# A decoder layer on one core: low parts of weights on VectorE, another pace of the inverse, tied gates, and other places for sums and tiles

## The chip, the cores and the metric

The kernel runs on one core of a Trainium2 chip. The metric is the device time of one execution in microseconds. The core has TensorE (PE; its weight loads are PEld), VectorE (DVE), ScalarE (ACT), GpSimd (POOL) and SyncE (SP), which run their own instruction queues and wait for one another by semaphores. DMAs are issued from the queues of SP, ACT and POOL.

## The reference

One layer of a decoder trunk, for 1024 positions of width 1024, in float32 (cut to what matters):

```python
h = rms_norm(x, norm1_g);  proj = h @ w_in
p_rwkv, p_sb, q_mem, gate_logits = split(proj)
y_a = rwkv7_branch(p_rwkv)                 # 8 heads x 64, delta-rule state, recurrence over time
y_b = stick_breaking_branch(p_sb)          # 8 heads x 64, strictly causal
y_m = memory_branch(q_mem, mem)            # 4 heads x 128, softmax over 256 memory tokens
gates = sigmoid(gate_logits)               # 3 branches x 1024
x = x + sum_b(gates_b * (y_b @ w_branch_b)) @ w_out
x = x + conv_ffn(x)                        # up 1024 -> 5632, causal depthwise conv of 3, silu(gate) * val, down 2816 -> 1024
```

## The kernel before, in words

**High and low parts.** TensorE multiplies in the fp32r format. Each operand is split into a high part (a copy rounded to fp32r, made on ScalarE) and a low part (the operand minus the high part). Every product is three matmuls: high by high, high by low, low by high (`mm3`, L102). For a weight, `split_raw` (L82) makes the high part `wh` on ScalarE (L83) and the low part `wl`, usually on GpSimd (L89); with `dve=True` it is made on VectorE (L86), behind the last fixed VectorE instruction. `split_w` (L96) loads a weight block of 128 x 1024 into a buffer `wr` and calls `split_raw`; `wr`, `wh` and `wl` have two buffers each.

**Order.** `pinned` (L119) keeps the instructions that go through it in program order on their engine and records the last one of each engine in `last_fixed`. `behind` (L127) puts one instruction after another on the same engine. All other instructions are placed by a scheduler, by priority. TensorE's order is that of the program.

**Fillers and main work.** A stream of items (`stream`, L852) is the filler: projections of the stick-breaking keys and queries, the gates (`gate_item`, L871), the memory's keys and values, the memory queries, later the branch products. An item is a block of 48 matmuls (8 steps of six) with hooks at some steps; the next item's weight is loaded and split when an item starts. `weave` (L1945) alternates the steps of a main generator with filler steps. Main generators are, in order, `rwkv_prep` (four pairs of heads p), `sb_attn` (stick-breaking attention, the first attention), `mem_attn` (attention to the memory, the second), `stage2` (the RWKV recurrence) and `group_norm`.

- `rwkv_prep` (L411): `decayed` (L528) is a product on GpSimd whose result TensorE transposes in `turned`.
- `sb_qk` (L891) gives, for a pair p of heads, a key item, a sum of squares of the keys (`k_ss`), a query item and hooks for the gate item behind it. `k_bc` broadcasts the keys' factors over TensorE (the transposed tile comes from `expand_heads`, L358), `k_split` makes high and low parts of the keys, `q_ss` sums the queries' squares on TensorE and calls `head_norm` (L816), which takes the sums out of a PSUM bank (`hn`, L822) and has GpSimd raise them to a power (L190).
- `sb_attn` (L953): for each of 64 units TensorE forms scores, ScalarE takes a sigmoid (L971), VectorE runs a scan (L977), TensorE transposes, ScalarE copies, TensorE multiplies by the values.
- `inverse` (L573): 62 steps of two VectorE instructions (L580, L582) invert triangular blocks in place, then 16 DMAs on GpSimd's queue (L589) write the result (`td`), with three generator steps for each. `run` advances it by `pace[0]` tenths of a step for each filler step: 8 from the first attention on. What is left of it is done behind the mark "mem". `stage2` reads `td`.
- `mem_attn` (L1183): for each of 8 units scores, a maximum on VectorE (L1201), an exponential on ScalarE (L1207), scaling, transposes and the product with the values.
- A gate item ends with two copies out of PSUM on ScalarE (L877), a product on VectorE (L878), later a sigmoid and a store.

**The feed-forward layer.** Up and down projections save multiplications by a two-by-two block scheme with seven products in place of eight. In `up_phase` (L1509) a pair n of column blocks has the products 1, 5, 6, 2, 7, 4, 3 (`step`), of 12 matmuls each; L1677 adds product 6 to a partial sum and so frees the bank that product 7 accumulates into; `conv` applies the convolution; `act_sums` (L1636) forms sums of the activated blocks (L1638) in a tile `sa` and stores them, a "not late" and a "late" half. `hl` (L1543) makes high and low parts of weight sums in tiles of tag `l4`, of which there are 16. In `down_phase` (L1806) each of the seven products is 11 steps f of 12 matmuls; `prep` loads and splits the operands three steps ahead (L1843 to L1846), `complete` adds the last sums into the residual tiles at the steps f = 0 to 3 of the next product, and `release` issues the stores at f = 5.

## Time and profile before

| | |
|---|---|
| runs shown | 1799.64, 1798.66, 1793.97 us (median 1798.66) |
| profiled execution | 1796.01 us; span from the first to the last instruction 1794.2 us |
| mean granted TensorE clock | 0.999 |
| TensorE, VectorE, ScalarE, GpSimd busy | 1778.1, 1176.6, 882.9, 737.2 us |
| first attention, main part | about 317 to 640 us from the span's start |
| second attention | about 671 to 745 us |
| recurrence on TensorE | from 792.6 us |
| up phase, down phase | about 1156 to 1580, 1580 to 1790 us |

A row of a profile gives a line of the kernel, an engine, an operation, the tile written <- the tiles read, and times in us unless marked ns. The ends of matmuls are modelled, so TensorE counts as busy for a little longer than it works. In a list of waits "PE g L117 <- DVE hn L822" reads: TensorE, about to write a tile g at L117, waited for VectorE's instruction on tile hn at L822.

### The profile page before, as it was taken

The page shows a single profiled execution, that of the slowest core. Times are in us where ns is not written, and L with a number is a line of the kernel's source. Part 1 is how long each engine was busy: PE and PEld are TensorE (multiplying, and loading weights), DVE is VectorE, ACT ScalarE, POOL GpSimd, SP SyncE. Part 2 cuts the span into 40 slices and gives each one's busy share as a digit, 9 for nine tenths or more (in the row PEclk, how much of TensorE's full clock was granted, in tenths as well). Part 3 has the DMA queues.
Part 4 walks back from the last instruction along what each step waited for, and adds up shares of the span by engine and source line. Part 5 has one row for each costly group of instructions (what it writes and reads, how often), then busy time and mean ns, then how long its engine had stood idle before and what let it go on. Part 6 is the DMA issues. An engine that isn't in the chain of part 4 may idle for free.

```text
span 1794.2 us, 27468 instructions
## 1 busy us (share of the span) xinstructions
PE 1778.1 (99%) x10481; PEld 1444.7 (81%) x10481; DVE 1176.6 (66%) x1670; ACT 882.9 (49%) x1667; POOL 737.2 (41%) x426
## 2 busy tenths in 40 slices
PE   9999999999999999999999999999999999999999
PEld 7777777878788887787777888887888888888887
DVE  5666655898987415233533782697767777785596
ACT  6544344465666636534556534464444445444343
POOL 1233252322222443122333321347777677635454
PEclk9999999999999999999999999999999999999999
DMA  4256574111111342557764662323322323396475
GB/s 185 73 168 194 177 252 133 55 53 45 51 59 65 124 144 68 181 184 252 275 232 162 224 215 102 118 89 123 100 88 98 120 91 120 112 324 225 143 245 201
DMA packets 120757, 263.39 MB, mean 147 GB/s; under 512 B 28329, under 2 KB 41129, under 8 KB 120498
## 3 DMA queue, kind: packets, MB, share of 16 engines
q1 hardware_dynamic: 82434, 193.31, 32.7%
q10 hardware_dynamic: 34416, 55.72, 8.5%
q0 software_dynamic: 3776, 12.62, 2.1%
q8 instruction: 82, 1.34, 0.3%
q14 instruction: 49, 0.40, 0.1%
HBM read 180.04 MB, written 81.53 MB: 146 GB/s over the span
## 4 chain that ended last, share of the span: by engine, by line
PE 90%; DVE 4%; POOL 2%; issue 1%; ACT 1%; DMA 1%; SPq 0%; ACTq 0%; DVEq 0%; POOLq 0%
PE mm L134 74%; PE g L134 13%; PE g L117 4%; POOL dw L1846 1%; DVE at L977 1%; DVE it L580 1%; DVE inst L582 1%; DMA at<-in_xT_dram 0%; DVE qk L923 0%; DVE qk L922 0%; DMA wr<-in_w_in_dram 0%; POOL wl L89 0%; DVE w L911 0%; POOL hf L190 0%; DMA qk<-vd 0%
## 5 line engine op out<-in xcount | busy, mean ns | idle before, releaser
L89 POOL TENSOR_TENSOR wl<-wr,wh 128x1024 fp32r<-128x1024 f32 x75 | 189.0, 2521 | 434.6 <-ACT wh L83 434.5
L134 PE MATMUL mm<-xhi,wh 128*128 128x512 f32 x784 | 261.2, 414 | 0.6 <-ACT w L928 0.4
L134 PE MATMUL mm<-xlo,wh 128*128 128x512 f32 x784 | 244.1, 393 | 0.2
L134 PE MATMUL mm<-xhi,wl 128*128 128x512 f32 x784 | 242.8, 391 | 0.2 <-POOL wl L89 0.2
L134 PEld LDWEIGHTS mm<-xlo,wh 128*128 128x128 f32 x784 | 147.4, 188 | 33.5 <-DVE xlo L219 1.0
L134 PEld LDWEIGHTS mm<-xhi,wl 128*128 128x128 f32 x784 | 147.5, 188 | 33.2 <-POOL wl L89 0.6
L134 PEld LDWEIGHTS mm<-xhi,wh 128*128 128x128 f32 x784 | 137.3, 190 | 30.5 <-issue 7.9
L83 ACT ACTIVATE wh<-wr 128x1024 fp32r<-128x1024 f32 x75 | 79.5, 1060 | 89.8 <-PE mm L134 67.5
L134 PE MATMUL mm<-dw,da 128*128 128x512 f32 x528 | 120.9, 390 | 0.0
L134 PE MATMUL mm<-BT,l 128*128 128x512 f32 x504 | 117.9, 390 | 0.3 <-POOL l L1547 0.3
L134 PEld LDWEIGHTS mm<-dw,da 128*128 128x128 f32 x528 | 99.0, 188 | 21.3 <-DVE da L1845 0.8
L1846 POOL TENSOR_TENSOR dw<-draw,dw 128x512 fp32r<-128x512 f32 x55 | 82.6, 1514 | 77.3 <-ACT dw L1844 76.0
L134 PEld LDWEIGHTS mm<-BT,l 128*128 128x128 f32 x504 | 94.6, 188 | 20.2 <-POOL l L1547 0.7
L134 PE MATMUL mm<-BT,wh 128*128 128x512 f32 x352 | 108.6, 390 | 1.7 <-DVE u L1677 1.7
L134 PE MATMUL mm<-B,wh 128*128 128x512 f32 x352 | 108.6, 390 | 0.0
L977 DVE TENSOR_TENSOR_SCAN at<-at,at 128x128 f32<-128x128 f32 (+3 forms) x64 | 91.1, 1428 | 23.3 <-ACT at L971 23.0
L1845 DVE TENSOR_TENSOR da<-draw,da 128x512 fp32r<-128x512 f32 x77 | 68.1, 894 | 50.4 <-ACT da L1843 50.0
L190 POOL TENSOR_TENSOR hf<-rs,half 128x16 f32<-128x16 f32 (+1 forms) x18 | 49.3, 2738 | 105.4 <-DVE rs L187 100.6
L134 PE MATMUL g<-dw,da 128*128 128x512 f32 x396 | 90.5, 390 | 0.4 <-POOL dw L1846 0.4
L1843 ACT ACTIVATE da<-draw 128x512 fp32r<-128x512 f32 x77 | 48.3, 629 | 82.6 <-PE mm L134 34.1
L134 PEld LDWEIGHTS g<-dw,da 128*128 128x128 f32 x396 | 74.3, 188 | 16.1 <-POOL dw L1846 0.8
L878 DVE TENSOR_TENSOR w<-w,rbc 128x1024 f32<-128x1024 f32 x24 | 48.3, 2012 | 56.1 <-ACT w L877 56.0
(342 smaller groups left out, 3963.4 us busy)
## 6 DMA issues: line engine op xcount, KB each, us to landing
wr<-in_w_in_dram SPq DMA_DIRECT2D x49, 512.0 KB, 3.8
draw<-actd SPq DMA_DIRECT2D x77, 256.0 KB, 3.0
at<-scr SPq DMA_DIRECT2D x28, 512.0 KB, 5.5
draw<-in_w_down_dram SPq DMA_DIRECT2D x55, 256.0 KB, 4.5
rw<-in_w_up_dram SPq DMA_DIRECT2D x22, 512.0 KB, 3.5
actd<-gall ACTq DMA_DIRECT2D x41, 256.0 KB, 3.2
gsd<-w ACTq DMA_DIRECT2D x20, 512.0 KB, 2.8
wr<-in_w_up_dram SPq DMA_DIRECT2D x18, 512.0 KB, 3.6
```

Of the source, the lines that this page charges most:

```text
L83: ins = self.nc.scalar.activation(hi, raw, AF.Copy)
L89: self.nc.gpsimd.tensor_tensor(lo, raw, hi.bitcast(F32), ALU.subtract)
L117: self.pinned(self.nc.tensor.transpose(out, in_, self.ident[:n, :n]))
L134: self.pinned(self.nc.tensor.matmul(*a, **k))
L190: nc.gpsimd.tensor_tensor(out, t[:, :n], self.half[:, :n], ALU.pow)
L580: self.pinned(nc.vector.tensor_tensor(tv, X[:, 0:s, s : s + 1].to_broadcast([128, s, n]), X[:, s : s + 1, s + 1 : 64].to_broadcast([128, s ...
L582: self.pinned(nc.vector.tensor_tensor(X[:, 0:s, s + 1 : 64], X[:, 0:s, s + 1 : 64], tv, ALU.add))
L878: nc.vector.tensor_tensor(g, g, self.rbc, ALU.mult)
L977: self.pinned(nc.vector.tensor_tensor_scan(sn[:, :W][:, ::-1], sn[:, :W][:, ::-1], self.smask[:, 1024 - W :][:, ::-1], 1.0, ALU.mult, ALU. ...
L1843: self.pinned(nc.scalar.activation(A[:, 0], a, AF.Copy))
L1845: self.pinned(nc.vector.tensor_tensor(A[:, 1], a, A[:, 0].bitcast(F32), ALU.subtract))
L1846: nc.gpsimd.tensor_tensor(Wt[:, 1], w, Wt[:, 0].bitcast(F32), ALU.subtract)
```

## The change

- `split_w` hands `low_dve` on to `split_raw`. It is set by a new entry of the item list, between the second and the third of the gates that follow the four key and query pairs, and taken back behind the mark "mem".
- `decayed` of the last pair (p = 3) is put behind the newest low part made on GpSimd.
- In the second attention (`late`) a gate's copies and its product go behind the last fixed instruction of their engine.
- For pair 0 `k_bc`, `k_split(0)` and `q_ss` come one step of six matmuls later.
- The inverse runs at 6 tenths from the first attention on and at 11 from the second on.
- `hl` for 512 columns puts both parts into one tile. The sums of the activated blocks 0 and 1 are formed at other products.
- In the down phase `complete` runs at f = 0, 2, 4, 6 and `release` at f = 8.

```diff
@@ split_raw
-            self.nc.gpsimd.tensor_tensor(lo, raw, hi.bitcast(F32), ALU.subtract)
+            self.last_wl = self.nc.gpsimd.tensor_tensor(lo, raw, hi.bitcast(F32), ALU.subtract)
         return hi, lo
+
+    def last(self, ins):
+        if self.late:
+            self.behind(ins, self.last_fixed[ins.ins.engine])
+        return ins
@@ split_w
-        return self.split_raw(raw, hi, lo)
+        return self.split_raw(raw, hi, lo, self.low_dve)
@@ startup
+        self.late = self.low_dve = False
@@ rwkv_prep, decayed
-            nc.gpsimd.tensor_tensor(
+            ins = nc.gpsimd.tensor_tensor(
                 self.c8(bp), self.c8(bk), pc[:, h * 8 : h * 8 + 8].unsqueeze(2).to_broadcast([128, 8, 128]), ALU.mult)
+            if p == 3:
+                self.behind(ins, self.last_wl)
@@ gate_item, fin
-                self.leave(nc.scalar.activation(g[:, h * 512 : (h + 1) * 512], pp[h], AF.Copy))
-            nc.vector.tensor_tensor(g, g, self.rbc, ALU.mult)
+                self.leave(self.last(nc.scalar.activation(g[:, h * 512 : (h + 1) * 512], pp[h], AF.Copy)))
+            self.last(nc.vector.tensor_tensor(g, g, self.rbc, ALU.mult))
@@ sb_qk
-        hooks = {1: lambda: k_split(1), 3 if p else 2: q_ss, 4: lambda: q_split(0), 6: lambda: q_split(1)}
-        kq = {4: k_bc, 5: lambda: k_split(0)}
+        hooks = {1: lambda: k_split(1), 3: q_ss, 4: lambda: q_split(0), 6: lambda: q_split(1)}
+        kq = {4: k_bc, 5: lambda: k_split(0)} if p else {5: k_bc, 6: lambda: k_split(0)}
@@ up_phase, hl
-            hi, lo = (pool.tile([128, n], F32R, name=self.nm(t), tag=t, bufs=16 if t == "l4" else 2) for t in tags)
+            if n == 512:
+                t = pool.tile([128, 2, n], F32R, name=self.nm("l"), tag="l4")
+                hi, lo = t[:, 0], t[:, 1]
+            else:
+                hi, lo = (pool.tile([128, n], F32R, name=self.nm(t), tag=t, bufs=16 if t == "l4" else 2) for t in tags)
@@ up_phase, step 6
                 if n > 2 and pairs[n - 1][2]:
-                    act_sums(pairs[n - 1][1], True)
+                    act_sums(pairs[n - 1][1], n > 4)
@@ up_phase, step 3
-                elif pairs[n][2]:
+                elif pairs[n][2] and n > 3:
                     act_sums(pairs[n][1], False)
@@ up_phase, loop over pairs
-                elif n == 3 and i in (5, 6, 7, 4):
-                    late, part = ((False, 0), (False, 1), (True, 0), (True, 1))[(5, 6, 7, 4).index(i)]
-                    act_sums(0, late, (part,))
+                elif n == 3 and i == 5:
+                    act_sums(0, False, (0,))
+                elif n == 3 and i == 6:
+                    act_sums(0, False, (1,))
+                    act_sums(0, True, (0,))
+                elif n == 3 and i == 7:
+                    act_sums(0, True, (1,))
+                elif n == 4 and i == 7:
+                    act_sums(1, True)
@@ down_phase
-            if f < 4:
-                complete(f)
-            elif f == 5:
+            if f < 8 and f % 2 == 0:
+                complete(f // 2)
+            elif f == 8:
                 release()
@@ run
-        items += [gate({0: prep[0], 5: prep[1]}), gate(), gate({2: prep[0], 6: prep[1]}), mss, *mv, *mk, mqi[0][0], mark("kv")]
+        items += [gate({0: prep[0], 5: prep[1]}), gate(), lambda: setattr(self, "low_dve", True), gate({2: prep[0], 6: prep[1]}), mss, *mv, *mk, mqi[0][0], mark("kv")]
...
-        pace[0] = 8
+        pace[0] = 6
         self.guard = True
         need("sb0")
         self.weave(self.sb_attn(qk, need), pump, 1.03, 0)
+        pace[0] = 11
         need("kv")
+        self.late = True
         self.weave(self.mem_attn(mq, need), pump, 1.6, 0)
         need("mem")
-        self.guard, self.last_fin = False, None
+        self.guard, self.last_fin, self.late, self.low_dve = False, None, False, False
```

## The prediction

> **What bounds the kernel now.** I read the page first, then the list of who waited for whom on TensorE, then the waits' own stretches.
>
> ```profile
> span 1794.2 us, 27468 instructions
> PE 1778.1 (99%) x10481; PEld 1444.7 (81%) x10481; DVE 1176.6 (66%) x1670; ACT 882.9 (49%) x1667; POOL 737.2 (41%) x426
> ```
>
> TensorE is busy for 1778.1 of 1794.2 us, and the change neither adds nor removes a matmul. So what can be won is only the time in which TensorE stands still. The waits of TensorE, longest first (engine and line that waits, whom it waited for, total us, times, longest), are these:
>
> ```profile
> PE g L117 <- DVE hn L822: 1.8, 1, 1.8
> PE mm L134 <- DVE u L1677: 1.7, 1, 1.7
> PE g L134 <- DVE hn L822: 1.5, 1, 1.5
> PE g L134 <- DVE qk L196: 1.5, 1, 1.5
> PE mm L134 <- POOL wl L89: 1.5, 2, 1.3
> PE g L117 <- DVE w L358: 0.7, 1, 0.7
> PE g L134 <- ACT at L1207: 0.6, 1, 0.6
> PE g L134 <- ACT w L929: 0.5, 1, 0.5
> PE mm L134 <- DVE qk L1171: 0.5, 1, 0.5
> PE g L134 <- DVE ys L648: 0.5, 1, 0.5
> PE mm L134 <- ACT w L928: 0.4, 1, 0.4
> PE g L134 <- POOL dw L1846: 0.4, 1, 0.4
> PE mm L134 <- POOL l L1547: 0.3, 1, 0.3
> ```
>
> They add up to 11.9 us in 14 waits, and each belongs to one place of the code. L196 (start), L1171 and L648 lie where the change does nothing: 2.5 us stay. To the other 9.4 us comes one stretch of slow clock. The columns are the stretch, its length, busy us (instructions) of TensorE, its weight loads, VectorE, ScalarE and GpSimd, granted clock, DMA share and GB/s:
>
> ```profile
> 676.40:679.90 3.50, 2.86 (x44) 2.31 (x43) 1.11 (x3) 3.06 (x8) 1.11 (x2) 1.00 0.55 143
> 679.90:683.40 3.50, 3.50 (x12) 2.83 (x12) 2.85 (x10) 0.95 (x3) 1.23 (x1) 0.51 0.14 49
> ```
>
> Right behind the 0.6 us wait for L1207 the clock is 0.51 for 3.5 us, which loses about 3.5 x 0.49 = 1.7 us. The ceiling of the whole change is so 9.4 + 1.7 = 11.1 us, 0.6% of the time.
>
> **The change part by part.**
>
> *GpSimd's order at the last RWKV pair* (`decayed` for p = 3 goes behind the newest weight's low part).
>
> ```profile
> 245.85 1.90 POOL L530 TENSOR_TENSOR it<-qk,pc 128x1024 f32<-128x1024 f32 x1 [6.40 <-DVE qk L417]
> 247.71 5.69 POOL L89 TENSOR_TENSOR wl<-wr,wh 128x1024 fp32r<-128x1024 f32 x2
> 258.49 1.03 PE L117 MATMUL g<-kon,it 128*128 128x128 f32 x8
> ```
>
> The 1.90 us product stands ahead of the low part for which TensorE waits 1.3 us. With the two exchanged that wait goes. The product then ends about one low part later, near 250, and its reader on TensorE comes at 258.49, so 8 us of projection hide it. **-1.3 us.**
>
> *The hooks of pair 0* (key broadcast, key split and query sum each one step of six matmuls later).
>
> ```profile
> 439.70 1.38 PE mm L134 x6
> 319.72 0.35 ACT L971 ACTIVATE at<-g,nf 128x128 f32<-128x128 f32 x1
> 324.89 0.42 DVE L977 TENSOR_TENSOR_SCAN at<-at,at 128x128 f32<-128x128 f32 x1
> ```
>
> A step of six is 1.38 us, longer than the 0.7 (L358) and 0.5 us (L929) that TensorE waits there: both go. What is late next is the query's factor, up to 1.38 us later: the first sigmoid (319.72) waits for it, but the scan that reads it starts 5 us later, held by VectorE's own queue. **-1.2 us.**
>
> *Fewer early inverse steps* (0.6 instead of 0.8 per step of the filler in the first attention, 1.1 in the second). The chain of the work that ended last, cut to the stretches ahead of the two waits for L822, has these shares by line (27 us from 436, 28 us from 358):
>
> ```profile
> by line: DVE it L580 20.3%; PE mm L134 19.9%; DVE at L977 18.8%; DVE inst L582 12.6%; DVE qk L923 9.1%; DVE qk L922 8.6%; DVE w L911 5.2%; PE g L117 2.9%; PE g L134 2.0%; issue 0.7%; DVE hn L822 0.4%
> by line: DVE at L977 29.3%; DVE it L580 18.4%; DVE inst L582 18.2%; DVE qk L923 8.8%; DVE qk L922 8.4%; DVE w L911 4.6%; DVE qk L939 4.6%; PE g L134 4.3%; DVE w L358 2.5%; PE g L117 1.2%; issue 0.9%; DVE hn L822 0.7%
> 316.00:600.00 284.00, 280.33 (x1923) 228.90 (x1921) 245.03 (x224) 169.98 (x322) 69.01 (x30) 1.00 0.18 58
> ```
>
> VectorE is busy for 245 of 284 us there, and hn, a tiny operation that frees a PSUM bank, stands behind its backlog. The inverse (L580 and L582) is 32.9% of 27 us = 8.9 us of the one chain and 36.6% of 28 = 10.2 us of the other. A quarter less takes 2.2 and 2.6 us out, more than the 1.8 and 1.5 us waited. **-3.3 us.** The 0.4 us for L928 (ScalarE) stays.
>
> The steps moved have to be done before the recurrence reads the inverse:
>
> ```profile
> L580 DVE TENSOR_TENSOR it<-inst x62: 226/945/3359, 284.3 to 588.0; 128x62 f32<-128x62 f32 x2, 128x122 f32<-128x122 f32 x2, 128x180 f32<-128x180 f32 x2, 128x236 f32<-128x236 f32 x2
> L589 POOL DMA_DIRECT2D td<-inst x16: 796/832/913, 588.9 to 699.8; - x16
> 792.59 0.52 PE L134 MATMUL g<-qk,at 64*64 64x64 f32 x12
> ```
>
> At 0.6 the 303.7 us of VectorE's part become 405. The first attention ends near 640 with 88% of it done, and the last 15 of 124 instructions follow at 1.1 by about 667. The 16 transfers behind them (48 steps, now 111 us at 0.8) take 81 at 1.1 and end near 748. The first reader comes at 792.59, so 45 us of filler hide this; without the cover the recurrence would start late by the same amount.
>
> *Low parts of the weights on VectorE.* The switch is set behind the third gate from the last key/query pair, so it covers the memory's eight half-products, four query projections and four gates, 16 low parts from about 600 on. "Both attentions" is thus the end of the first and the second; in most of the first GpSimd keeps them.
>
> ```profile
> L89 POOL TENSOR_TENSOR wl<-wr,wh x75: 2360/2401/3891, 41.4 to 1044.8; 128x1024 fp32r<-128x1024 f32 x75
> L230 DVE TENSOR_TENSOR wl<-wr,wh x2: 1218/1222/1227, 6.1 to 9.9; 128x1024 fp32r<-128x1024 f32 x2
> 600.00:785.00 185.00, 183.73 (x1119) 149.98 (x1118) 64.84 (x111) 90.86 (x180) 65.21 (x44) 0.99 0.43 138
> ```
>
> GpSimd loses 16 x 2.40 = 38.4 us, VectorE gets 16 x 1.22 = 19.5 us, in a stretch where it is idle for 120 us. Each low part is ready 1.2 us sooner, so the remaining 0.2 us of TensorE's waits for L89 goes. Against it stands a new wait: VectorE takes its queue in order, and a low part that stands there before its high part is copied holds the attention's maxima and scans behind it. Nothing in the trace shows this exactly; the bounds are 0 and 19.5 us (every one exposed in full). The nearest row is the query's low part, which waits for ScalarE in the same way: 8 of L1171 in this stretch cost TensorE 0.5 us in all. I take twice that for 16: **-0.2 + 1.0 us.**
>
> The rule against this part is in the Trainium skill, "TensorE: Matmul & The Clock Gate", section "Architectural detail": ScalarE and VectorE are strict FIFOs. The first rival below is what it would do here.
>
> *Tied gates* (in the second attention copies and products of a gate follow the last fixed instruction of their engine). Behind a late copy waits the next user of its two PSUM banks. The row for L928, 0.4 us for such a copy, over three gates gives 0 to 1.2 us; ScalarE is 49% and VectorE 35% busy there, so I take 0. As nothing then gets ahead of the attention's exponentials, the 0.6 us for L1207 goes, and with it the window that fell to 2.86 busy us of 3.5: **-0.6 - 1.7 us.** The same page, section "What's actually happening", wants a wholly idle window of some 3.4 us before the clock is halved. Here a window with 82% busy came before it, so the measured drop decides; by the rule the wait did not cause it, the 1.7 us stay and the sum below is 1.7 us smaller.
>
> *Up phase.* The chain ahead of the wait for L1677:
>
> ```profile
> 1242.96 1.98 DVE gall L1638
> 1246.56 0.69 DVE u L1677
> 1237.00:1265.00 28.00, 26.01 (x114) 21.00 (x113) 25.29 (x36) 13.27 (x19) 24.57 (x16) 1.00 0.40 132
> ```
>
> Sums of blocks 0 and 1 (L1638) lie together ahead of the L1677 that frees the bank. The change takes block 0's last sums one product earlier and block 1's behind L1677. That clears the 3.6 us between the two rows against 1.7 waited. What is late next are the additions at L1690, with a product of 12 matmuls (2.76 us) as cover. The halves hl makes for 512 columns take one slot of 16 instead of two, so the low part at L1547 need not wait for a slot. **-1.7 - 0.3 us.**
>
> *Down phase.* In the stretch ahead of the wait for L1846 VectorE has no idle time:
>
> ```profile
> 1732.40:1746.40 14.00, 14.00 (x64) 11.59 (x63) 13.86 (x17) 4.62 (x8) 6.19 (x4) 1.00 0.67 224
> ```
>
> Two final sums in each of four successive steps make 13.86 us of work where four steps of twelve matmuls last 4 x 2.76 = 11.0. In every second step they fit. **-0.4 us.** The results leave three steps (8 us) later, two steps ahead of the next loads into their tiles; I take 0, and 0 to 3 us as the price if they collide.
>
> *Sum:* -1.3 - 1.2 - 3.3 - 0.2 + 1.0 - 0.6 - 1.7 - 2.0 - 0.4 = **-9.7 us.** The profiled execution took 1796.0 us (its span and 1.8 around it), so 1786.3. It lies 2.7 below the median of the three runs (1793.97 to 1799.64); the mean of all four is 1797.1. I add that 1.1: **1787.5 us.**
>
> **The rivals.**
>
> *Slower: low parts at the head of VectorE's queue.* Each may wait there for its high part (about 1.06 us on ScalarE, after TensorE has left the buffer) and then run 1.22 us, while maxima and scans wait and TensorE runs out of its four "g" banks. For it speaks that TensorE has no slack in this stretch (183.73 of 185), against it the 120 idle us of VectorE and only 0.5 us lost to L1171. At 2.28 us for half of the 16 it costs 18 us instead of 1: 1787.5 + 17 = 1804.5. It makes the kernel slower from about 1 us per low part on.
>
> *The waits of the first attention come back.*
>
> ```profile
> 394.47 3.36 DVE L580 TENSOR_TENSOR it<-inst 128x962 f32<-128x962 f32 x1
> 394.31 2.49 POOL L89 TENSOR_TENSOR wl<-wr,wh 128x1024 fp32r<-128x1024 f32 x1 [4.42 <-ACT wh L83]
> ```
>
> GpSimd's low parts stay in most of that attention, and an inverse step that runs beside one lasts 3.36 us, where the median was 0.945. If this backlog, not the number of steps, makes hn late, 3.3 us return, and with the clock's 1.7 the kernel takes 1792.5. It is also the case in which the change does less than it says.
>
> *More slow windows of the clock.* Rearranged small matmuls may drop the clock elsewhere, 1.7 us each: with the one kept and two new ones, 1787.5 + 5.1 = 1792.6.
>
> **How the numbers follow.** About 0.3% (5.4 us) can be told from no change, so faster means below 1793.3 and slower above 1804.1. The forecast has 0.62 (1782 to 1792), the returning waits 0.22, the clock 0.07, the queue's head 0.09. Of the second half ends above 1793.3, of the third two parts of seven, of the first 0.02, of the last 0.01 stays below 1804.1: faster 0.76, within 0.16, slower 0.08. The range from 1780 (the ceiling of 11.1 us from 1794, with 3 us for what restarts cost) to 1797 leaves out the queue's case and a tail of the second.
>
> **What would show it.** In the profile after: no wait for L89 near 250, none for L358 and L929 near 300, none for hn; the wait for L1677 and the one for dw gone; clock 1.00 near 680; 16 low parts of about 1.22 us on VectorE between 600 and 790; last td transfer before 760. I am wrong if TensorE shows new waits for VectorE's maxima or low parts between 600 and 790, or for hn at other pairs.

## The result and the profile after

The changed kernel took 1800.70 us (median of 10 runs, 1800.02 to 1802.16), the kernel before 1797.04 us (10 runs, 1793.97 to 1799.64): ratio 1.0023, 95% interval 1.0013 to 1.0032. It is slightly slower, 13 us from the 1787.5 forecast and above the range. Of 71 executions of the kernel before that were timed beside the experiments below, 23 had a mean granted TensorE clock below 1.000 and took 2.8 us longer in the median; of the ten of the changed kernel none had. The profiled execution of the changed kernel took 1800.42 us. The top of its page:

```profile
span 1798.6 us, 27428 instructions
PE 1779.3 (99%) x10481; PEld 1440.9 (80%) x10481; DVE 1191.4 (66%) x1687; ACT 881.3 (49%) x1667; POOL 700.6 (39%) x409
```

The same 10481 matmuls; GpSimd lost 36.6 us of work and VectorE got 14.8. Lines below L89 are shifted: L134 is now L139, L1547 L1559, L1638 L1650, L1677 L1689, L1845 L1863. The longest of TensorE's waits:

```profile
PE mm L139 <- DVE u L1689: 5.8, 7, 0.8
PE mm L139 <- POOL l L1559: 1.5, 1, 1.5
PE g L139 <- DVE qk L202: 1.5, 1, 1.5
PE mm L139 <- POOL wl L1559: 1.4, 1, 1.4
PE mm L139 <- DVE da L1863: 1.2, 1, 1.2
PE mm L139 <- DVE wl L86: 0.7, 2, 0.5
PE g L122 <- ACT at L997: 0.6, 1, 0.6
PE mm L139 <- DVE xlo L225: 0.6, 1, 0.6
```

Both waits for hn are gone, and so are those for L358, L929, L89, L1207 and dw. In their place stand nine waits in the up phase (8.7 us: the rows for L1689 and L1559), one in the down phase (da, L1863) and three short ones in the attention part (L86 and L997, 1.3 us). Where the time went is seen best by comparing the start of the matmul of the same number in TensorE's order in the two traces (after minus before, us; the times are those of before):

| up to | 251 | 303 | 580 | 638 | 699 | 1224 | 1552 | 1750 | end |
|---|---|---|---|---|---|---|---|---|---|
| offset | -1.4 | -2.5 | -7.1 | -4.7 | -7.2 | -7.4 | +3.5 | +2.8 | +4.4 |
| gained or lost in the stretch | -1.4 | -1.1 | -4.6 | +2.4 | -2.5 | -0.2 | **+10.9** | -0.7 | +1.6 |
| forecast | -1.3 | -1.2 | -3.3 | +0.8 | -2.3 | 0 | **-2.0** | -0.4 | 0 |

The first 1224 us went much as forecast (-7.4 against -7.3). The up phase, forecast as a gain of 2.0, lost 10.9 us. The -2.3 forecast up to 699 holds the 1.7 us of the slow clock.

**What happens in the up phase.** Pair 10, before, on ScalarE, GpSimd and VectorE in turn (start us, us, engine line operation, out<-in; in brackets the idle time ahead and who ended it). Product 6 ends at 1358.95, where the first matmul of product 2 starts; product 7 follows 12 matmuls later, at 1361.67 in this trace:

```profile
1358.98 1.06 ACT L1546 ACTIVATE l<-it 128x1024 fp32r<-128x1024 f32 x1 [2.78 <-PE mm L134]
```

```profile
1360.12 2.40 POOL L1547 TENSOR_TENSOR l<-it,l 128x1024 fp32r<-128x1024 f32 x1 [5.29 <-ACT l L1546]
```

```profile
1358.55 1.42 DVE L1638 TENSOR_TENSOR gall<-gall 128x512 f32<-128x512 f32 x2
1359.90 0.68 DVE L1677 TENSOR_TENSOR u<-mm,p 128x512 f32<-128x512 f32 x1
```

The same pair after, where that end lies at 1354.04:

```profile
1346.18 1.05 ACT L1558 ACTIVATE l<-it 128x1024 fp32r<-128x1024 f32 x1
```

```profile
1354.12 2.40 POOL L1559 TENSOR_TENSOR l<-it,l 128x1024 fp32r<-128x1024 f32 x1 [5.62 <-PE mm L139]
```

```profile
1353.56 3.51 DVE L1650 TENSOR_TENSOR gall<-gall 128x512 f32<-128x512 f32 x2
1357.00 0.68 DVE L1689 TENSOR_TENSOR u<-mm,p 128x512 f32<-128x512 f32 x1
```

ScalarE's high part of the weight sums goes 8 us before the end of product 6 instead of right behind it, so GpSimd's low part begins 0.08 us behind that end instead of 1.17. VectorE forms two sums there; the second now begins 0.16 us behind the start of GpSimd's low part and ends 0.5 us behind its end: the two sums took 1.42 us and take 3.51. The u addition behind them frees the bank for product 7. It now ends at 1357.68, product 7 starts at 1357.74, and TensorE has waited. It happens in seven of the eight even pairs from 6 to 20, those whose sums stand there; the waiting product starts about 0.98 us late each time, and such a pair takes 20.4 us where it took 19.05 (shorter delays where one product follows another make the rest). In the eighth, pair 12, the sum began first and GpSimd's low part was held instead; there stands the 1.4 us wait for wl.

The pair ahead of it, after, has no sums there, and its u addition reads its first operand from PSUM (VectorE, then GpSimd):

```profile
1335.12 0.69 DVE L1689 TENSOR_TENSOR u<-mm,p 128x512 f32<-128x512 f32 x1 [0.70 <-PE mm L139]
```

```profile
1335.00 2.40 POOL L1559 TENSOR_TENSOR l<-it,l 128x1024 fp32r<-128x1024 f32 x1 [5.65 <-PE mm L139]
```

It runs beside the same low part and takes 0.69 us. The Trainium skill, "SBUF — State Buffer", section "SBUF: two separate sides", says this: VectorE and GpSimd share a pair of ports by an exclusive lock held for a whole instruction, and of VectorE's instructions those with two SBUF inputs contend for it with a GpSimd instruction that reads SBUF. Both rows agree: the sum with two SBUF inputs is held to the end of the low part, the addition with one is not.

### The profile page after: what moved, and what is told of

Its sections match the earlier page's. It is cut to its first block, busy times and chain, and to the rows that moved or that the text cites. A ratio compares the mean times of both kernels' runs of the same rounds, so it can differ in the third digit from the quotient of the medians.

```text
span 1798.6 us, 27428 instructions
## 1 busy us (share of the span) xinstructions
PE 1779.3 (99%) x10481; PEld 1440.9 (80%) x10481; DVE 1191.4 (66%) x1687; ACT 881.3 (49%) x1667; POOL 700.6 (39%) x409
## 4 chain that ended last, share of the span: by engine, by line
PE 50%; DVE 5%; issue 5%; POOL 4%; ACT 2%; DMA 1%; ACTq 0%; DVEq 0%; POOLq 0%; SPq 0%
PE mm L139 42%; PE g L139 7%; POOL dw L1864 1%; PE g L122 1%; DVE g L1633 1%; DVE g L1634 1%; DVE gall L1639 1%; POOL l L1559 1%; POOL it L1576 1%; POOL it L1580 1%; ACT wh L1558 0%; POOL wl L1559 0%; POOL rw L1586 0%; DVE gall L1650 0%; DMA draw<-actd 0%
## 5 line engine op out<-in xcount | busy, mean ns | idle before, releaser
L89 POOL TENSOR_TENSOR wl<-wr,wh 128x1024 fp32r<-128x1024 f32 x58 | 148.0, 2552 | 367.9 <-ACT wh L83 360.2
L139 PE MATMUL mm<-xhi,wh 128*128 128x512 f32 x784 | 260.6, 413 | 0.9 <-ACT xhi L222 0.5
L139 PE MATMUL mm<-xlo,wh 128*128 128x512 f32 x784 | 243.6, 392 | 0.7 <-DVE xlo L225 0.6
L139 PE MATMUL mm<-xhi,wl 128*128 128x512 f32 x784 | 242.2, 390 | 0.0
L139 PEld LDWEIGHTS mm<-xlo,wh 128*128 128x128 f32 x784 | 147.0, 188 | 34.0 <-DVE xlo L225 1.6
L139 PEld LDWEIGHTS mm<-xhi,wl 128*128 128x128 f32 x784 | 147.2, 188 | 32.6
L139 PEld LDWEIGHTS mm<-xhi,wh 128*128 128x128 f32 x784 | 136.5, 189 | 30.7 <-issue 7.9
L139 PE MATMUL mm<-dw,da 128*128 128x512 f32 x528 | 121.4, 390 | 1.2 <-DVE da L1863 1.2
L83 ACT ACTIVATE wh<-wr 128x1024 fp32r<-128x1024 f32 x75 | 79.5, 1060 | 81.7 <-PE mm L139 63.2
L139 PE MATMUL mm<-BT,l 128*128 128x512 f32 x504 | 118.0, 389 | 1.5 <-POOL l L1559 1.5
L139 PEld LDWEIGHTS mm<-dw,da 128*128 128x128 f32 x528 | 98.8, 188 | 23.2 <-DVE da L1863 2.8
L139 PE MATMUL mm<-BT,wh 128*128 128x512 f32 x352 | 109.4, 392 | 5.9 <-DVE u L1689 5.8
L139 PEld LDWEIGHTS mm<-BT,l 128*128 128x128 f32 x504 | 94.5, 188 | 21.6 <-POOL l L1559 1.9
L139 PE MATMUL mm<-B,wh 128*128 128x512 f32 x352 | 108.9, 391 | 0.0
L1863 DVE TENSOR_TENSOR da<-draw,da 128x512 fp32r<-128x512 f32 x77 | 69.4, 910 | 49.4 <-ACT da L1861 48.7
L139 PE MATMUL g<-dw,da 128*128 128x512 f32 x396 | 90.2, 389 | 0.0
L139 PEld LDWEIGHTS g<-dw,da 128*128 128x128 f32 x396 | 74.3, 188 | 15.4
L139 PEld LDWEIGHTS mm<-BT,wh 128*128 128x128 f32 x352 | 65.5, 188 | 22.6 <-DVE u L1689 8.7
```

Of the source, the lines that this page charges most:

```text
L83: ins = self.nc.scalar.activation(hi, raw, AF.Copy)
L89: self.last_wl = self.nc.gpsimd.tensor_tensor(lo, raw, hi.bitcast(F32), ALU.subtract)
L139: self.pinned(self.nc.tensor.matmul(*a, **k))
L1863: self.pinned(nc.vector.tensor_tensor(A[:, 1], a, A[:, 0].bitcast(F32), ALU.subtract))
```

## The experiments

Theory: the attention part is as good as forecast, and the single tile in `hl` costs some 11 us because it moves GpSimd's low part to a time at which it holds VectorE's sum ahead of the bank's reader. First rival: the changed places of the sums do it. Second rival: the attention part, through GpSimd's or VectorE's altered load. All medians below stand beside runs of the kernel before made with them on the same chip (1795.07 to 1795.78 us); ratios are to these.

### Parts alone and parts undone

**att_only**: the kernel before with the attention part of the change alone.

```diff
 after
-            if n == 512: ... (hl as before)
-  act_sums at other products (as before)
-  complete at f = 0, 2, 4, 6, release at f = 8 (as before)
```

> The kernel before with only the part of the change that lies ahead of the feed-forward layer (low parts on VectorE, pace of the inverse, tied gates, hooks of pair 0, decayed behind the low part); hl, the sums of the activated blocks, complete and release as before. Theory: the loss arises in the up phase by the one tile for both halves in hl, so this kernel keeps the 7.2 us that the changed kernel was ahead at 1230 us: 1790 us, no wait longer than 0.2 us at L1689 but the one of 1.8 us near pair 4 that the kernel before has. Rival: the attention's new order shifts the phase of GpSimd and VectorE in the up phase, and the waits of about 1 us in every second pair are there too: 1798 to 1800 us.

1789.69 us, ratio 0.9962 (0.9948 to 0.9976). The attention part is a gain; the offset at 699 is -6.2 and stays there through the up phase, so the second rival falls.

**hl_back**: the changed kernel with two tiles in `hl`.

```diff
-            if n == 512:
-                t = pool.tile([128, 2, n], F32R, name=self.nm("l"), tag="l4")
-                hi, lo = t[:, 0], t[:, 1]
-            else: ...
+            hi, lo = (pool.tile([128, n], F32R, ...) for t in tags)
```

> The changed kernel with two tiles again for the two parts in hl at 512 columns, all else as changed. Theory (the tile lets GpSimd start the low part of the weight sums as product 6 ends, and that holds VectorE's sum ahead of L1689): the seven waits of 0.8 us at L1689 and those of 1.5 and 1.4 us for POOL at L1559 go, 1790 us within 2. Rival (the other places of the sums of blocks 0 and 1 put VectorE behind for the rest of the phase): the waits stay, 1799 to 1801 us.

1789.62 us, 0.9964 (0.9951 to 0.9977): these lines alone cost about 11 us, and the list of waits has no u addition in it any more. One 1.5 us wait for GpSimd's l stayed, so it belongs to the places of the sums, not to the tile.

**hl_only**: the kernel before with the one tile in `hl` (the diff above the other way round).

> The kernel before with nothing but the one tile in hl at 512 columns. Theory: it alone costs what the up phase lost, about 1 us in each of eight pairs and some 3 us for two waits for POOL's low parts: 1807 us within 2. Rival (the places of the sums are the cause): 1797, as before.

1806.84 us, 1.0058 (1.0042 to 1.0073). The longest wait is now

```profile
PE mm L134 <- DVE u L1681: 9.0, 9, 2.5
```

of which 1.7 us stood there before. Undoing and adding agree, and the first rival falls.

### Why the one tile does it

**hi_late**: hl_only, with ScalarE's copy put behind a later one; no work and no tile differs.

```diff
 hl (weight sums of pairs 4 to 21)
+            ins = keep(nc.scalar.activation(hi, src, AF.Copy))
+            self.behind(ins, self.last_u1)      # ScalarE's copy of product 2
 loop over pairs
-                    prep2(nxt)                  # at i == 6
+                    sums2(nxt)                  # at i == 6
+                    the rest of prep2(nxt)      # at i == 2, behind u1_first
```

> The kernel before with one tile in hl, and in pairs 4 to 21 ScalarE's high part of the weight sums put behind ScalarE's copy of product 2 of the pair ahead, the product that follows product 6. The amount of work and the tiles are those of hl_only; only the time at which GpSimd can begin the low part moves. Theory (the loss comes from the time at which GpSimd's 2.40 us low part begins: beside VectorE's sum ahead of the bank's reader): the low part begins 3 us or more behind the end of product 6, the second sum takes 0.69 us again, the waits for the u addition of hl_only (9.0 us in 9) go and the time is back at about 1797, within 2 us. Rival A (one shared tile costs by something else, such as a reader of the one half waiting for the other): the waits stay and the time is 1804 or more. Rival B (the low part then holds other work of VectorE, or is late itself): other waits of 6 us or more in all, 1802 to 1806.

1796.18 us, ratio 1.0001 (0.9991 to 1.0012): the whole loss is gone, 10.7 us by the place of one copy. In pair 10, on GpSimd and on VectorE:

```profile
1365.03 2.41 POOL L1553 TENSOR_TENSOR l<-it,l 128x1024 fp32r<-128x1024 f32 x1
```

```profile
1358.34 1.42 DVE L1646 TENSOR_TENSOR gall<-gall 128x512 f32<-128x512 f32 x2
1359.68 0.69 DVE L1685 TENSOR_TENSOR u<-mm,p 128x512 f32<-128x512 f32 x1
```

The low part lies 6 us behind the end of product 6, the two sums take 1.42 us again, and between 1250 and 1580 TensorE waits for nothing. The start of GpSimd's instruction, moved by nothing but the place of the copy ahead of it, is the cause.

**low_vector**: hl_only, with this low part on VectorE from pair 3 on.

```diff
-            w = hl(st[n, "s"], ..., eng=engine(n)[1])
+            w = hl(st[n, "s"], ..., eng=engine(n)[1] if n < 3 else nc.vector)
```

> The kernel before with the one tile in hl, and the low part of the weight sums (l<-it) of pairs 3 and up on VectorE in place of GpSimd. Theory (GpSimd's low part, started 0.1 us behind product 6, holds the sum of activated blocks for 2.8 us in place of 0.7): nothing of GpSimd's lies there any more, the sum takes 0.7 us, and the waits of about 1 us at L1681 in every second pair go: 1796 to 1800 us, though VectorE has 1.2 us more to do in each pair. Rival (VectorE has too much to do): its waits get longer by about the added 1.2 us: 1812 us or more.

1821.18 us, 1.0140 (1.0125 to 1.0155); the theory's number was missed, the rival's held:

```profile
PE mm L134 <- DVE u L1681: 23.0, 9, 4.5
```

The low part now stands itself ahead of the u addition, and GpSimd's other work still holds sums (1.6 to 1.8 us where 0.69 is free). VectorE has no room at that place, whoever fills it.

**sums_behind**: the changed kernel with the sums of all blocks behind the bank's reader, as the change has it for block 1.

```diff
-                    act_sums(pairs[n - 1][1], n > 4)              # at product 6
+                    act_sums(pairs[n - 1][1], False)              # at product 6
-                elif n == 4 and i == 7:
-                    act_sums(1, True)
+                elif n > 3 and i == 7 and pairs[n - 1][2]:
+                    act_sums(pairs[n - 1][1], True)
```

> The changed kernel, with the one tile kept, in which the sums of every block from 1 on are formed where the change forms those of block 1: the first half behind L1689 in step 6, the second in step 7 of the next pair. Theory (a sum ahead of L1689, held by GpSimd's low part, is what delays the bank): the waits at L1689 go, those for POOL's low parts (2.9 us) stay: 1792 us within 3. Rival (VectorE as a whole is too slow with the new order of GpSimd): waits of the same size at L1689, L1702 or L1703: 1799 or more.

1805.06 us, 1.0049 (1.0033 to 1.0065): missed. The u addition is free, but GpSimd is late in its turn:

```profile
PE mm L139 <- POOL wl L1559: 11.1, 7, 1.8
```

Clearing VectorE's queue did not clear the conflict; why wl became late was not followed further.

**slot_held and slot_kept**: why does one tile let ScalarE copy early? GpSimd's idle time ahead of L1547 and L1551 (all its low parts from 1250 to 1560), before and in hl_only, ended so:

```profile
its engine sat idle before it (us, times) until:
  ACT l L1546: 77.7, 17
```

```profile
its engine sat idle before it (us, times) until:
  PE mm L134: 88.4, 16
```

Before, GpSimd waited for ScalarE's copy, which itself waited for TensorE to leave a slot. With one slot less in use per pair the copy finds a free one, and GpSimd waits for TensorE, that is for the slot of its own result. Both slots come free with product 6; the 1.06 us copy between them used to put the low part behind VectorE's sums. To show it, a slot is taken away again:

```diff
 hl_only, loop over pairs
+            if n == 4:
+                hold = self.pool_l.tile([128, 1024], F32, name="hold", tag="l4")
+                nc.gpsimd.memset(hold[:, :2], 0.0)
+            elif n == len(pairs) - 2:
+                held = self.small("held", [128, 2])
+                ins = nc.gpsimd.tensor_tensor(held, hold[:, :2], hold[:, :2], ALU.add)
+                self.behind(ins, self.last_low)      # slot_kept only
```

> The kernel before with the one tile in hl, and with one of the 16 tiles of tag l4 held unused from pair 4 to pair 20 of the up phase (two GpSimd instructions on two columns). Theory (the tile's gain of a free slot is what lets the high part of the weight sums go early, so that the low part starts 0.1 us behind product 6 and not 1.2 us): with the slot gone again the low part starts 1.2 us behind product 6, and the waits of about 1 us at L1681 go from pair 6 on: 1797 to 1799 us. Rival (high and low part in one tile are freed together, and that shifts the order): the waits stay, 1806 us.

1813.42 us, 1.0098 (1.0081 to 1.0115), with the low part still at +0.08. Alone it proves nothing: the read that should hold the tile was placed right behind the write,

```profile
L1782 POOL MEMSET hold<- x1: 94/94/94, 1247.8 to 1247.8; 128x2 f32 x1
L1785 POOL TENSOR_TENSOR held<-hold x1: 583/583/583, 1247.9 to 1247.9; 128x2 f32<-128x2 f32 x1
```

so the slot was held for under 1 us. In slot_kept the read is tied to a low part of pair 19 and runs at 1556.6.

> The kernel before with one tile in hl, and one tile of the l4 pool kept unused from pair 4 to pair 19 (one small write and one small read on GpSimd, the read tied behind a low part of pair 19). Theory (the freed slot lets ScalarE's copy go early; the low part's own slot comes free at the end of product 6 as before): with the slot taken away the copy waits for product 6 again and starts at about +0.03 us, the low part at +1.17, GpSimd's idle time ahead of its low part ends by ScalarE's copy, and the waits for the u addition between 1260 and 1530 go: about 1797 to 1799. Rival (the shared tile itself does it, whatever the number of slots): copy at about -8, low part at +0.08, nine waits of 0.98 us, 1805 to 1808.

In pairs 5 to 19 the copy starts at +0.03 and the low part at +1.17, TensorE has no wait between 1280 and 1530, and GpSimd (1270 to 1530) waits for ScalarE again:

```profile
its engine sat idle before it (us, times) until:
  ACT l L1550: 71.6, 14
```

So it is the number of slots, not the shared tile. The time, however, was 1806.65 us, 1.0055 (1.0036 to 1.0075): not the 1797 to 1799 of the theory, but inside the rival's 1805 to 1808. The kernel to lay beside it is slot_held, which differs in the one line that ties the read. There the copy starts 8 us ahead of the end of product 6 and the low part at +0.08 in the same pairs, and it takes 6.8 us more; the intervals of the two ratios do not overlap. What the two have in common costs the rest. Against before, slot_held loses 1.5 us ahead of 251 and 2.9 between 853 and 1224, slot_kept 1.4 and 4.1 (0.6 of it a wait), where no line of the kernel differs and long before the tile is written. Between 1160 and 1224 us a matmul starts 231 ns (median) behind the one before it in both, 227 in the kernel before, at a granted clock of 1.00. The steps between matmuls that changed by no more than 0.1 us add up to 11.7 us lost in slot_held and 10.9 in slot_kept, about all that slot_kept loses. So it is not the kept slot that slows the matmuls; which part of what was added in both kernels (two GpSimd instructions, two tiles) does it stays open.

**after_hi_late**: the changed kernel with hi_late's edit.

> The changed kernel with the same one edit: the high part of the weight sums behind the copy of product 2. Theory: the 7.0 us of waits for the u addition go, and the time is that of the changed kernel with two tiles in hl, 1789.6, within 2 us. Rival (GpSimd's low parts come too late, as when the sums went behind the bank's reader): waits for GpSimd's wl or l of 6 us or more, 1798 or more.

1789.64 us, 0.9965 (0.9952 to 0.9978), as expected; the u addition is gone from the list, the wait for l is 0.5, and the one for da is 1.4.

### The attention part

**pace_only**: the kernel before with the new pace alone.

```diff
-        pace[0] = 8
+        pace[0] = 6
...
         need("sb0")
         self.weave(self.sb_attn(qk, need), pump, 1.03, 0)
+        pace[0] = 11
```

> The kernel before with only the pace of the inverse changed (6 in the first attention, 11 from its end on). Theory (the inverse's share of VectorE's backlog makes hn late): the waits of 1.8 and 1.5 us for hn go, TensorE is 3.5 us ahead at 580 us, and nothing of it is lost behind: 1792.5 us. Rival (GpSimd's low parts, not the inverse, make the backlog): half or more of the two waits stays: 1794 to 1796 us.

1798.26 us, 1.0017 (1.0008 to 1.0027). The waits for hn went as the step said (offset -4.5 at 580), but others came:

```profile
PE g L134 <- ACT at L1207: 3.9, 1, 3.9
PE mm L134 <- POOL wl L89: 3.3, 2, 2.0
```

Between 580 and 638 it lost 2.6 us (the 2.0 us wait for wl lies there), and between 699 and 853 5.5: the 3.9 us wait, and right behind it 3.5 us at a granted clock of 0.51. Alone, the pace gives back more than it wins; neither the theory's 1792.5 nor the rival's 1794 to 1796 held.

**no_ties**: att_only without the tied gates.

```diff
-        self.late = True
+        self.late = False
```

> The kernel before with the attention part alone, without the tied gates of the second attention. Theory (the ties keep the exponentials ahead of the gates' copies once the filler runs at 1.1): the waits that the pace alone brought back come again (3.9 us for ScalarE's exponentials, 5.6 us lost between 699 and 853), 1793 to 1796. Rival (the ties do nothing, the low parts or GpSimd's order kept that stretch free): 1789 to 1791, and no loss between 699 and 853.

1793.37 us, 0.9986 (0.9976 to 0.9995), 3.7 us behind att_only. Between 699 and 853 it lost 2.9 us, by

```profile
PE g L139 <- ACT at L1215: 2.3, 1, 2.3
```

which is L1207 of before. The ties are what keeps the exponentials ahead of the gates at the faster pace.

**no_low**: att_only without the low parts on VectorE.

```diff
-  lambda: setattr(self, "low_dve", True),
```

> The kernel of att_only (attention's part of the change, feed-forward layer as before) without the switch for VectorE's low parts. Theory (low parts on VectorE stand in its queue ahead of scans and cost TensorE the 3.4 us that att_only lost between 580 and 638 us): the loss goes to under 1 us: 1787 us. Rival (the inverse's late steps or the ties of the gates cost it): 1790 us, and the loss between 580 and 638 us stays.

1789.84 us, 0.9963 (0.9950 to 0.9976), the same as att_only, so the theory's 1787 was missed. Its waits between 570 and 640 us:

```profile
PE mm L139 <- POOL wl L89: 1.4, 1, 1.4
PE g L122 <- DVE at L985: 0.6, 1, 0.6
```

In att_only stand 1.3 us for VectorE's wl and 0.6 for L997 instead. Between 580 and 638 no_low loses 2.0 us where att_only loses 3.4, but it loses 1.2 more between 1060 and 1224 (0.8 of it a wait for L1354 near 1064). Moving the low parts swaps one wait for another.

### The down phase

**down_only** and **release_late**: the kernel before with the down phase's edits, and with the later release alone.

```diff
 both
             if f < 4:               # down_only: f < 8 and f % 2 == 0
                 complete(f)         # down_only: f // 2
-            elif f == 5:
+            elif f == 8:
                 release()
```

> The kernel before with the down phase's part alone: one final sum in every second step, and the release of the results at the ninth step. Theory: the 0.4 us for dw goes, and 1 to 2 us are lost near 1768, because the loads into the tiles of the results wait for their stores; waits for da or dw of 1 to 2 us there, 1796 to 1798. Rival (the wait for da is no matter of the release): no wait over 0.5 us in the last 40 us, 1795 to 1796.

> The kernel before with one edit: the results of the down phase leave at the ninth step of a half-product instead of the sixth; the sums stay where they were. Theory (the loads of the next residual into the same tiles wait until the stores have landed, and the operands' loads stand behind them on SP's queue): the loads of the last half go some 5 to 8 us later than the 1755.3 to 1757.9 of before, TensorE waits 1 to 3.5 us for da there, and nothing is lost ahead of 1750; 1797 to 1800. Rival (the spread of the sums made that loss): no wait for da over 0.5 us, 1795 to 1796.

1796.76 us, 1.0012 (1.0000 to 1.0023), and 1800.86 us, 1.0029 (1.0019 to 1.0039). The release alone costs a little more than the 1797 to 1800 of the theory. Its trace, the fastest of ten executions, loses 2.1 us from 1750 to 1772, as expected, and 1.2 between 1552 and 1750, which was not; the rest of the difference of the medians is in no kept trace. The way there may be another than the theory's, too. The trace of release_late, ScalarE:

```profile
1757.57 0.86 ACTq L1863 DMA_DIRECT2D out_dram<-dx  x2
1758.53 0.63 ACT L1843 ACTIVATE da<-draw 128x512 fp32r<-128x512 f32 x1 [4.32 <-DMA out_dram<-it]
```

and VectorE:

```profile
1759.20 0.69 DVE L1845 TENSOR_TENSOR da<-draw,da 128x512 fp32r<-128x512 f32 x1 [3.35 <-ACT da L1843]
1759.81 6.89 DVE L1908 TENSOR_TENSOR keep<-keep 128x512 f32<-128x512 f32 x4
1766.62 0.68 DVE L1845 TENSOR_TENSOR da<-draw,da 128x512 fp32r<-128x512 f32 x1
```

The stores stand on ScalarE's queue ahead of its copies and wait there for earlier transfers; ScalarE is held 4.32 us (1.91 before), VectorE 3.35, and the four last residual sums (L1908, 6.89 us) then stand ahead of the next da, for which TensorE waits 1.5 us. Before, the same sums began at 1757.99 and the da came at 1763.70. The loads on SP's queue were late as well (1759.5 to 1763.6 instead of 1755.3 to 1757.9), as the theory had it. The chain that the profile draws for 1752 to 1772 passes through them into the third of the four sums, but VectorE shows no idle time ahead of that sum. So the path through ScalarE is read from the rows, not shown by a run. In down_only's trace TensorE waits 3.2 us for da at the same place, against 1 to 2 expected, and then has a slower clock (0.74 and 0.77 in two stretches of 3.5 us). That execution also lost 3.8 us between 1324 and 1408, in the up phase, where it differs from before in nothing: a second wait for the u addition of L1677, 1.9 us, and a slower clock behind it (0.73 and 0.78). It was the slowest of ten; the interval of its runs says more than that one trace.

**late_no_down**: after_hi_late with the down phase of before.

```diff
-            if f < 8 and f % 2 == 0:
-                complete(f // 2)
-            elif f == 8:
+            if f < 4:
+                complete(f)
+            elif f == 5:
                 release()
```

> after_hi_late with the down phase of before (both edits out). Theory: the 1.4 us for da and about 0.4 more come back, the 0.9 us that the spread sums won are lost again: 1788 to 1789.5, 0.5 to 1 us ahead of after_hi_late in the trace. Rival (the loss near 1770 comes from the earlier start alone, as the 1.2 us of the attention part alone): the same time as after_hi_late within 0.4 us, with a wait for da or dw of about 1 us there.

1787.70 us, ratio 0.9961 (0.9947 to 0.9975): the lowest median of all versions, 7.5 us below the kernel before. Its trace loses 0.3 us from 1750 to 1772 where after_hi_late loses 1.8, and it has no wait for da. The intervals of the two ratios overlap, so it is the traces that tell them apart.

## Why the prediction was wrong, step by step

- **Order at the last RWKV pair: right.** -1.4 us for -1.3. GpSimd after the change; the low part now stands first:

```profile
244.98 2.40 POOL L89 TENSOR_TENSOR wl<-wr,wh 128x1024 fp32r<-128x1024 f32 x1 [5.50 <-ACT wh L83]
248.00 1.90 POOL L536 TENSOR_TENSOR it<-qk,pc 128x1024 f32<-128x1024 f32 x1 [0.63 <-DVE qk L423]
```

- **Hooks of pair 0: right.** -1.1 for -1.2; nothing became late in their place.
- **Fewer early inverse steps: right in mechanism, larger in size.** -4.6 for -3.3, with both hn waits gone. The rival "waits come back" fell. The step did not see what the new pace costs later: pace_only loses 2.6 us between 580 and 638 and 5.5 between 699 and 853. The last transfer of the result was issued in time, at 717.9 us; the estimate for their end was 748:

```profile
L597 POOL DMA_DIRECT2D td<-inst x16: 796/811/960, 657.5 to 717.9; - x16
```

- **Low parts on VectorE: the sum about right, and worth nothing.** 17 of them were moved,

```profile
L86 DVE TENSOR_TENSOR wl<-wr,wh x17: 1194/1223/1227, 576.9 to 745.2; 128x1024 fp32r<-128x1024 f32 x17
```

  and the stretch from 580 to 638 lost 2.4 us for 0.8 forecast. Most of this loss comes with the pace: it was 2.0 in no_low and 2.6 in pace_only, which move no low part, and 3.4 in att_only. The slower rival, low parts at the head of VectorE's queue at 18 us, fell: waits for wl L86 are 0.7 us.
- **Tied gates: they matter, for a reason the step did not have.** It gave them 0.6 us for L1207. At the old pace that was all there was; at the new one they save 2.9. The step judged each edit by the waits of before, and did not see that one edit opens the wait that another closes.
- **The slow clock at 680: real, but not in every execution.** The step put 1.7 us down to the wait for L1207 and counted them as a sure gain. Eight kept traces are unchanged at that place (before, hl_only, hi_late, low_vector, slot_held, slot_kept, down_only, release_late), and all have the 0.6 us wait. In two of them, before and slot_kept, the clock drops behind it; in the other six it stays at 1.00. First release_late, then slot_kept:

```profile
675.90:679.40 3.50, 2.86 (x44) 2.29 (x44) 1.16 (x3) 3.01 (x8) 1.16 (x2) 1.00 0.55 147
679.40:682.90 3.50, 3.50 (x19) 2.97 (x18) 2.80 (x10) 0.95 (x4) 1.18 (x1) 1.00 0.13 46
```

```profile
679.00:682.50 3.50, 2.89 (x45) 2.63 (x45) 0.80 (x3) 3.37 (x8) 0.80 (x2) 0.99 0.61 163
682.50:686.00 3.50, 3.50 (x11) 2.77 (x10) 3.08 (x11) 0.95 (x5) 1.53 (x1) 0.52 0.08 29
```

  Unchanged there, hl_only, hi_late, release_late and down_only all gained 1.1 to 1.2 us in that stretch against the first profile. So about 1.1 of the -2.5 us in the table is the luck of that profile. But such drops are no matter of that one place. Eight of the 17 kept traces have eleven of them, each about 3.5 us at half the clock, and each shortly behind a wait of TensorE: 0.6 us here in two traces, 1.8 to 4.5 us in the others (3.9 in pace_only). Other waits of up to 2.3 us have none behind them. The step was right that a drop can follow a wait, and wrong to count it as certain. The Trainium skill, "TensorE: Matmul & The Clock Gate", section "What's actually happening", by which the clock is halved after an idle window of about 3.4 us, does not agree with these traces: nine of the eleven waits were shorter.
- **Up phase: the step that failed.** "The halves hl makes for 512 columns take one slot of 16 instead of two, so the low part at L1547 need not wait for a slot", put at -0.3 us, cost 10.9 us with the rest of the phase and 11 alone. The low part still waits for a slot. What no longer waits is ScalarE's copy ahead of it, and that removed the 1.06 us that kept GpSimd off VectorE's sums. The rest of the step was half right: the 1.7 us for L1677 near 1246 went, but a 1.5 us wait for GpSimd's l, which hl_back shows to come from the sums' places, took most of it.
- **Down phase: sizes.** The 13.86 us that the step laid against four steps of 11.0 are VectorE's whole work in a stretch of 14 us, in which TensorE did 64 matmuls, more than five steps; they show that VectorE had no idle time, not that it was a quarter too slow. The spread sums gave -0.7 for -0.4. The release "two steps ahead of the next loads" was taken at 0 with a price of up to 3 us; the stretch lost 1.6. Not all of this need be the release: att_only, which has it as before, loses 1.1 us there too. release_late's rows show a way through ScalarE's queue; in the changed kernel the same rows stand in the same order (ScalarE idle 1.83 us around the dx stores, the four sums 6.90 us), which was read there and not tried apart.

No rival in the prediction was that of the up phase, although its own rows held the piece: an inverse step of VectorE (128x962) lasted 3.36 us beside a GpSimd low part, while the steps next to it, of 950 and 972 columns, took 1.12 and 1.14. That was applied to the first attention only. (The prediction's last sum, 1786.3 and 1.1, is 1787.4 and not 1787.5; nothing hangs on it.)

## What to carry to other kernels

A wait on an engine that is not the bottleneck can be what keeps two other instructions apart. Before a slot, a buffer or a queue is freed, ask which instruction will start earlier, and lay its new time against VectorE's work with two SBUF inputs if it runs on GpSimd. Judge a slow clock, and any single stall, by more than one execution, and judge edits that shift work in time together, since one can open the wait that the next one closes.

## What the runs showed of the hardware

- A VectorE sum of 128 x 512 from two SBUF operands took 0.69 us alone and 2.8 us when it began 0.16 us behind a GpSimd operation of 2.40 us; an addition with one operand in PSUM took 0.69 beside the same operation.
- TensorE's clock fell to about half for about 3.5 us shortly behind some of its waits: eleven times in 17 traces, behind waits of 0.6 to 4.5 us. The same 0.6 us wait was followed by it in two traces of eight.
- Two kernels with the same small addition (two GpSimd instructions on two columns, two tiles) had slower matmuls from the start on: 231 ns from start to start where the kernel before had 227, 11 to 12 us in all, at an unchanged granted clock. One of them held its tile for under 1 us, the other for 300 us. Why is open.
